# A conformer layer on one core: another order of products in the ffns' first block, and other PSUM banks for the memory values

## The chip, the cores and the metric

The kernel runs on one core of a Trainium2 chip. The metric is device time in microseconds (us); lower is better. TensorE (PE in the profile) multiplies, VectorE (DVE) and ScalarE (ACT) do elementwise work and read and write PSUM, GpSimd (POOL) makes a few powers, SyncE (SP) issues DMAs. PSUM has eight banks of 128 x 512 words; a matmul adds into one of them.

## The reference

One layer over 512 rows of 1024 columns, in float32: half a SwiGLU ffn, a mixer of three attention branches with gates, half a second ffn, a norm.

```
def swiglu(h, wg, wu, wd):
    return (jax.nn.silu(h @ wg) * (h @ wu)) @ wd

def memory_attention(q, mk, mv):
    sc = jnp.einsum('bshd,bmhd->bhsm', q, mk).astype(jnp.float32) * (d ** -0.5)
    p = jax.nn.softmax(sc, axis=-1)
    return jnp.einsum('bhsm,bmhd->bshd', p.astype(mv.dtype), mv).reshape(b, s, h * d)

x = x + 1/2 * SwiGLU(RMSNorm(x))
h = RMSNorm(x)
y = sum_i sigmoid(h W_g + b_g)_i * (o_i W_branch_i);  x = x + y W_out
x = x + 1/2 * SwiGLU(RMSNorm(x))
x = RMSNorm(x)
```

D_FF is 2816, so each ffn has 22 tiles of 128 hidden columns. Memory has 256 tokens; its keys and values are one product of the normed memory rows each, and keys and queries are normed per head.

## The kernel before

Every float32 factor is split into a high and a low half (`split`, L76 to L78: ScalarE casts, VectorE subtracts, so that "hi" is ready first and "lo" after it), and a product is three matmuls: hi by hi, lo by hi, hi by lo (`mm3`, L108 to L112).

**The ffn** (`ffn`, from L346) goes through the hidden tiles in blocks of 4, 6, 6 and 6 (`CHUNKS`). Two hidden tiles make an `Item`. Its two by two block product of gate and up weights is computed in Strassen's way, with seven products numbered 1 to 7 instead of eight. Each is 24 matmuls of 256 columns (`mm7`, L364). Their left operands are sums of parts of the normed rows (`mhi`, `mlo`), their right ones sums of weight quarters, which VectorE makes and splits (`Item.prep`, L390). Products 1, 6, 7 and 4 add one after the other to the same bank, `self.y` (tag `s`); products 5 and 3 add to `self.z` (tag `p` or `o`); product 2 has a bank of tag `g`. Between two additions to `y` the intermediate value is read out: `snap` (L415 to L418) is a ScalarE copy of the bank, after products 1, 6 and 7. The next product to the same bank waits for it. `gated` then makes silu of one part by the other, and `done` (L435) splits the result of a hidden tile into `gh` and `gl`, the operands of the down projection.

The down projection has two halves of 512 output columns (`dh`). For each, a chunk (L513 to L524) multiplies two hidden tiles: 24 matmuls of 512 columns into four banks. Chunk 0 of the first half is put ahead of the last item's products 4 and 3 (`end`).

The written order of a block is a list of jobs; `run_jobs` (L334) prepares the weights of jobs ahead of their use, as far as a ring of six weight blocks goes, and then runs the job. Each job's matmuls stand in a `tc.manual_schedule` of their own: within it TensorE's order is as written, while between jobs the framework's scheduler may put the matmuls of one job between those of another, and it does. In the first block of four tiles, with items A and B, the written order is A1 A2 B1 B2, A6 A5 A7 A4 A3, B6 B5 B7, chunk 0, B4 B3, chunk 2, then the second half's chunks. In the same block the left operands are still being made (`Operands`, rows, L201 to L250), and the memory rows are normed.

**Memory** (L618 to L651) comes between the first ffn and the mixer. `rows_product` (L584) multiplies in four chunks of weights (`mwh`, `mwl`), with accumulators for two tiles of 128 tokens. The keys' two accumulators are the two `s` banks. `norm4` (L604) takes squares (ScalarE), sums (`hss`, VectorE), a power (POOL), and scales; `heads_T` (L611) transposes the result through a `t` bank. The values' accumulators are the same two `s` banks, so their first matmul waits until the norm has read the keys. `PLAN_C0` is a list for the first step of the mixer that says in what turn projections (p), gate products (f) and the parts of memory's attention (c.qt, c.sc, ...) are issued.

Of the kernel before, what the change touches and what calls it, by code (L numbers as in the profile page):

```python
# [11 lines left out]
F32 = mybir.dt.float32  # L12
# [6 lines left out]
P = 128  # L19
# [7 lines left out]
NMT = NM // P  # L27
# [4 lines left out]

PLAN_C0 = "p2 c.qt p2 c.sc p2 f4 c.sc2 p3 f2 c.qt f2 c.pt f4 c.pv"
PLAN_C = "c.sc f1 p2 u.ot c.ot p2 u.pt c.sc2 p2 u.qt p3 c.qt f1 u.sc f1 c.pt f1 u.pv f1 c.pv"
# [13 lines left out]
def layer_kernel(ctx: ExitStack, tc: tile.TileContext, a: dict, out: bass.AP):  # L48
# [11 lines left out]
    def bank(tag):  # L60
        return pp.tile([P, 512], F32, tag=tag, name="ps_" + tag, bufs=BANKS[tag])
# [272 lines left out]
    def run_jobs(jobs, ring):  # L334

        made = alive = 0
        for n, job in enumerate(jobs):
            while made < len(jobs) and (made <= n or alive + jobs[made].blocks <= ring):
                alive += jobs[made].blocks
                jobs[made].got = jobs[made].prep() if jobs[made].prep else None  # L340
                made += 1
            with tc.manual_schedule(engines={mybir.EngineType.PE}):
                job.run(job.got)
            alive -= job.blocks

    def ffn(pre, x_sb, ops, fp, after, raws=None, before_last=None, after_half=None):  # L346
# [122 lines left out]
        ft = 0  # L469
        for n, nf in enumerate(CHUNKS):  # L470
# [4 lines left out]
            order = []  # L475
# [3 lines left out]
            else:  # L479
                order += [(items[0], 1), (items[0], 2)]  # L480
            for i, item in enumerate(items):
                order += [(item, 6), (item, 5), (item, 7)]
                if i + 1 < len(items) and not (ft == 0 and i == 0):
                    order += [(items[i + 1], 1)]
                if ft == 0 and i == 0:
                    order += [(item, 4), (item, 3)]
                elif i + 1 < len(items):
                    order += [(item, 4), (item, 3), (items[i + 1], 2)]
            jobs = [product(*o) for o in order]
# [3 lines left out]
            for dh in range(2):  # L493
# [31 lines left out]
                else:  # L525
                    run_jobs(jobs, RING)
                    jobs = []
# [83 lines left out]
    def heads_T(yn, dst, cols):  # L611

        ps = bank("t")
        for h in range(4):
            nc.tensor.transpose(ps[:, h * P:(h + 1) * P], yn[:, h * P:(h + 1) * P], ident)
        split(heads(ps, 4), dst[0][:, :, cols], dst[1][:, :, cols])
# [5 lines left out]
    mkT = [base.tile([P, 4, NM], F32R, tag="w4", name=n, bufs=2) for n in ("mkh", "mkl")]  # L622
    mk_ps = rows_product([bank("s") for _ in range(NMT)], mT, a["w_mem_kv"], 0, **mem_w)
    for t in range(NMT):
        yn = mem_pool.tile([P, 512], F32, tag="mk", name="mk", bufs=3)
        sq = mem_pool.tile([P, 512], F32, tag="mk", name="mksq", bufs=3)
        heads_T(norm4(mk_ps[t], yn, sq, gck), mkT, slice(t * P, (t + 1) * P))
    cq_ps = rows_product([bank(t) for t in ("p", "g", "g", "o")], h2, a["w_in"], 3072)
# [3 lines left out]
    for t in range(NT):  # L632
        sq = mem_pool.tile([P, 512], F32, tag="mk", name="cqsq", bufs=3)
        norm4(cq_ps[t], c_rows[:, t, :], sq, gcq)

    lam = mem_pool.tile([P, 512], F32, tag="mk", name="lam", bufs=3)
    la = lam[:, 0:256].rearrange("p (u v d) -> p u v d", u=2, v=2)
# [9 lines left out]
                            op0=ALU.add, op1=ALU.subtract)  # L647
    mv_ps = rows_product([bank("s") for _ in range(NMT)], mT, a["w_mem_kv"], 512, **mem_w)
    mv = base.tile([P, NMT, 512], F32, tag="kx", name="mv", bufs=2)
    for t in range(NMT):  # L650
        nc.scalar.copy(out=mv[:, t, :], in_=mv_ps[t])  # L651
    memp.__exit__(None, None, None)
    mix_in["mTp"].__exit__(None, None, None)
# [500 lines left out]
```

## Time and profile before

| | us |
|---|---|
| median of 3 runs | 1267.36 (1266.86 to 1268.57) |
| the profiled execution | 1268.73 |
| its span | 1266.9 |
| TensorE busy | 1228.1 (97%) |
| VectorE busy | 843.0 (67%) |
| ScalarE busy | 596.8 (47%) |

The mean granted clock of TensorE is 0.986 of full speed. The first block of the first ffn runs until 98.16 us, the memory stage from about 409 to 447 us, the first block of the second ffn from 905 to 986.5 us. Idle time in brackets at the end of a row is that of the row's engine just before the instruction, with what ended it. All times are from the span's start.

### The profile page before, as it was taken

The page shows a single profiled execution, that of the slowest core. Times are in us where ns is not written, and L with a number is a line of the kernel's source. Part 1 is how long each engine was busy: PE and PEld are TensorE (multiplying, and loading weights), DVE is VectorE, ACT ScalarE, POOL GpSimd, SP SyncE. Part 2 cuts the span into 40 slices and gives each one's busy share as a digit, 9 for nine tenths or more (in the row PEclk, how much of TensorE's full clock was granted, in tenths as well). Part 3 has the DMA queues.
Part 4 walks back from the last instruction along what each step waited for, and adds up shares of the span by engine and source line. Part 5 has one row for each costly group of instructions (what it writes and reads, how often), then busy time and mean ns, then how long its engine had stood idle before and what let it go on. Part 6 is the DMA issues. An engine that isn't in the chain of part 4 may idle for free.

```text
span 1266.9 us, 19640 instructions
## 1 busy us (share of the span) xinstructions
PE 1228.1 (97%) x7808; PEld 1119.2 (88%) x7808; DVE 843.0 (67%) x1377; ACT 596.8 (47%) x1115; POOL 106.2 (8%) x108
## 2 busy tenths in 40 slices
PE   7889999999999899999999999999989999999997
PEld 7779989989987799999999999888887998998996
DVE  7977667667664756667765664554697776766753
ACT  7534525435443455554554544442464452542543
POOL 1100000000000301111121121111000000000002
PEclk8899999999999899999999999999989999999999
DMA  6532423323333413212221321145143242332311
GB/s 222 174 103 82 135 84 107 127 79 122 102 123 117 123 39 109 88 42 84 88 88 54 93 88 38 63 146 186 34 135 115 70 134 97 101 125 76 123 44 67
DMA packets 53084, 127.57 MB, mean 101 GB/s; under 512 B 10112, under 2 KB 10624, under 8 KB 52992
## 3 DMA queue, kind: packets, MB, share of 16 engines
q1 hardware_dynamic: 52416, 125.27, 31.1%
q8 instruction: 61, 1.00, 0.3%
q10 hardware_dynamic: 576, 1.05, 0.2%
q14 instruction: 31, 0.25, 0.1%
HBM read 122.11 MB, written 4.19 MB: 100 GB/s over the span
## 4 chain that ended last, share of the span: by engine, by line
PE 91%; DVE 4%; ACT 1%; DMA 1%; POOL 1%; issue 1%; SPq 0%; POOLq 0%; DVEq 0%; ACTq 0%
PE ps_s L373 19%; PE ps_g L110 9%; PE ps_g L112 9%; PE ps_g L111 9%; PE ps_o L373 5%; PE ps_p L110 5%; PE ps_p L112 5%; PE ps_p L111 4%; PE ps_p L373 4%; PE ps_g L373 4%; PE ps_s L110 3%; PE ps_s L111 3%; PE ps_s L112 3%; PE ps_o L906 2%; PE ps_s L874 2%; PE ps_t L722 1%
## 5 line engine op out<-in xcount | busy, mean ns | idle before, releaser
L77 ACT CAST whi<-wraw 128x1024 fp32r<-128x1024 f32 (+1 forms) x120 | 119.1, 993 | 144.6 <-PE ps_s L373 74.1
L78 DVE TENSOR_TENSOR wlo<-wraw,whi 128x1024 fp32r<-128x1024 f32 (+1 forms) x120 | 137.9, 1151 | 67.8 <-ACT whi L77 65.1
L373 PE MATMUL ps_s<-mhi,whi 128*128 128x256 f32 x496 | 140.3, 283 | 8.1 <-ACT snap L417 7.9
L373 PE MATMUL ps_s<-mlo,whi 128*128 128x256 f32 x496 | 139.3, 281 | 0.0
L373 PE MATMUL ps_s<-mhi,wlo 128*128 128x256 f32 x496 | 138.3, 281 | 0.6 <-DVE wlo L78 0.6
L373 PEld LDWEIGHTS ps_s<-mhi,whi 128*128 128x128 f32 x496 | 94.6, 191 | 10.6 <-ACT snap L417 9.5
L77 ACT CAST whi<-quarter 128x1024 fp32r<-128x1024 f32 x54 | 56.8, 1052 | 96.4 <-PE ps_o L112 22.4
L373 PEld LDWEIGHTS ps_s<-mlo,whi 128*128 128x128 f32 x496 | 94.7, 191 | 0.9 <-DVE mlo L78 0.2
L373 PEld LDWEIGHTS ps_s<-mhi,wlo 128*128 128x128 f32 x496 | 94.5, 191 | 0.9 <-DVE wlo L78 0.8
L110 PE MATMUL ps_p<-whi,hh 128*128 128x384 f32 (+1 forms) x264 | 95.0, 360 | 0.0
L112 PE MATMUL ps_p<-whi,hl 128*128 128x384 f32 (+1 forms) x264 | 89.6, 340 | 0.0
L111 PE MATMUL ps_p<-wlo,hh 128*128 128x384 f32 (+1 forms) x264 | 89.0, 337 | 0.0
L78 DVE TENSOR_TENSOR wlo<-quarter,whi 128x1024 fp32r<-128x1024 f32 x54 | 66.0, 1222 | 23.9 <-ACT whi L77 23.9
L110 PE MATMUL ps_g<-hh,fh 128*128 128x512 f32 x192 | 78.1, 407 | 0.0
L112 PE MATMUL ps_g<-hh,fl 128*128 128x512 f32 x192 | 75.5, 393 | 0.1
L111 PE MATMUL ps_g<-hl,fh 128*128 128x512 f32 x192 | 74.9, 390 | 0.0
L859 DVE CAST kx<-ps_t 128x256 fp32r<-128x256 f32 x32 | 13.6, 425 | 84.6 <-PE ps_t L857 84.6
L121 POOL TENSOR_TENSOR rsh<-msh,mhalf 128x4 f32<-128x4 f32 x38 | 45.2, 1191 | 277.5 <-DVE msh L127 225.8
L78 DVE TENSOR_TENSOR fl<-wraw,fh 128x768 fp32r<-128x768 f32 x48 | 50.0, 1042 | 24.0 <-ACT fh L77 24.0
L77 ACT CAST fh<-wraw 128x768 fp32r<-128x768 f32 x48 | 39.9, 833 | 37.7 <-PE ps_g L111 22.4
L724 ACT COPY pT<-ps_t 128x512 f32<-128x512 f32 (+3 forms) x56 | 23.5, 452 | 69.3 <-PE ps_t L722 69.3
L110 PEld LDWEIGHTS ps_p<-whi,hh 128*128 128x128 f32 x264 | 50.4, 191 | 1.6
(416 smaller groups left out, 3691.7 us busy)
## 6 DMA issues: line engine op xcount, KB each, us to landing
wraw<-in_ffn_w SPq DMA_DIRECT2D x88, 512.0 KB, 3.8
wraw<-in_ffn_wd SPq DMA_DIRECT2D x44, 512.0 KB, 3.9
wraw<-in_w_u SPq DMA_DIRECT2D x32, 384.0 KB, 3.2
wraw<-in_w_gb SPq DMA_DIRECT2D x32, 384.0 KB, 3.1
wraw<-in_w_gf SPq DMA_DIRECT2D x16, 384.0 KB, 3.1
wraw<-in_w_mem_kv SPq DMA_DIRECT2D x8, 512.0 KB, 4.1
wraw<-in_w_out SPq DMA_DIRECT2D x8, 512.0 KB, 4.8
x_sb<-in_x SPq DMA_DIRECT2D x4, 512.0 KB, 7.0
```

The lines of the kernel that those rows point to most:

```text
L77: nc.scalar.copy(out=hi, in_=raw)
L78: (engine or nc.vector).tensor_tensor(out=lo, in0=raw, in1=f32(hi), op=ALU.subtract)
L110: nc.tensor.matmul(ps, lhsT=st[0], rhs=mv[0], start=first, stop=False)
L111: nc.tensor.matmul(ps, lhsT=st[0], rhs=mv[1], start=False, stop=False)
L112: return nc.tensor.matmul(ps, lhsT=st[1], rhs=mv[0], start=False, stop=last)
L121: nc.gpsimd.tensor_tensor(out=rs, in0=ms, in1=mhalf[:, :n], op=ALU.pow)
L373: nc.tensor.matmul(ps[:, c], lhsT=x, rhs=y, start=first and j + k + n == 0, stop=k == 3 and n == 2, skip_group_check=True)
L722: nc.tensor.transpose(ps[:, j * P:(j + 1) * P], pt[:, j * P:(j + 1) * P], ident)
L724: nc.scalar.copy(out=pT[:, :n * P], in_=ps[:, :n * P])
L859: nc.vector.tensor_copy(out=un.kx[:, :, qs], in_=heads(p2[:, 0:256], 2))
L874: nc.tensor.matmul(out_, lhsT=q, rhs=k, start=j == 0, stop=j == 1)
L906: nc.tensor.matmul(o[:, vs], lhsT=pT[:, j * P:(j + 1) * P], rhs=un.v[:, j, vs], start=j == 0, stop=j == i)
```

## The change

The first block's list of products is written in another order, all jobs of a list stand in one `manual_schedule`, so that TensorE follows the written order across jobs, too; the memory values accumulate in the two `t` banks, and the keys are transposed after the values' product; and the squares get buffers of their own. `PLAN_C0` is rewritten.

```diff
--- before.py
+++ after.py
@@ -30,7 +30,7 @@
 AHEAD = 600
 
 
-PLAN_C0 = "p2 c.qt p2 c.sc p2 f4 c.sc2 p3 f2 c.qt f2 c.pt f4 c.pv"
+PLAN_C0 = "p6 c.qt p3 f4 c.sc f4 c.sc2 f2 c.qt f1 c.pt f1 c.pv"
 PLAN_C = "c.sc f1 p2 u.ot c.ot p2 u.pt c.sc2 p2 u.qt p3 c.qt f1 u.sc f1 c.pt f1 u.pv f1 c.pv"
 PLAN_A = "c.sc p2 c.ot c.sc2 p3 u.pt p2 u.qt u.ot p2 c.pt f2 u.sc f1 u.pv c.pv f3"
 PLAN_B = "p5 u.pt p2 u.qt u.ot p2 f1 u.sc f1 u.pv f4"
@@ -334,14 +334,14 @@
     def run_jobs(jobs, ring):
 
         made = alive = 0
-        for n, job in enumerate(jobs):
-            while made < len(jobs) and (made <= n or alive + jobs[made].blocks <= ring):
-                alive += jobs[made].blocks
-                jobs[made].got = jobs[made].prep() if jobs[made].prep else None
-                made += 1
-            with tc.manual_schedule(engines={mybir.EngineType.PE}):
+        with tc.manual_schedule(engines={mybir.EngineType.PE}):
+            for n, job in enumerate(jobs):
+                while made < len(jobs) and (made <= n or alive + jobs[made].blocks <= ring):
+                    alive += jobs[made].blocks
+                    jobs[made].got = jobs[made].prep() if jobs[made].prep else None
+                    made += 1
                 job.run(job.got)
-            alive -= job.blocks
+                alive -= job.blocks
 
     def ffn(pre, x_sb, ops, fp, after, raws=None, before_last=None, after_half=None):
 
@@ -478,14 +478,15 @@
                 order += [(items[0], 1), (items[0], 2), (items[1], 1), (items[1], 2)]
             else:
                 order += [(items[0], 1), (items[0], 2)]
-            for i, item in enumerate(items):
-                order += [(item, 6), (item, 5), (item, 7)]
-                if i + 1 < len(items) and not (ft == 0 and i == 0):
-                    order += [(items[i + 1], 1)]
-                if ft == 0 and i == 0:
-                    order += [(item, 4), (item, 3)]
-                elif i + 1 < len(items):
-                    order += [(item, 4), (item, 3), (items[i + 1], 2)]
+            if ft == 0:
+
+                order += [(items[0], 6), (items[0], 5), (items[0], 7), (items[1], 6), (items[0], 4), (items[0], 3),
+                          (items[1], 5), (items[1], 7)]
+            else:
+                for i, item in enumerate(items):
+                    order += [(item, 6), (item, 5), (item, 7)]
+                    if i + 1 < len(items):
+                        order += [(items[i + 1], 1), (item, 4), (item, 3), (items[i + 1], 2)]
             jobs = [product(*o) for o in order]
             end = [product(items[-1], 4), product(items[-1], 3)]
 
@@ -621,19 +622,20 @@
         nc.sync.dma_start(out=g, in_=a[f"c_{n}_norm"].partition_broadcast(P))
     mkT = [base.tile([P, 4, NM], F32R, tag="w4", name=n, bufs=2) for n in ("mkh", "mkl")]
     mk_ps = rows_product([bank("s") for _ in range(NMT)], mT, a["w_mem_kv"], 0, **mem_w)
+    mk = []
     for t in range(NMT):
-        yn = mem_pool.tile([P, 512], F32, tag="mk", name="mk", bufs=3)
-        sq = mem_pool.tile([P, 512], F32, tag="mk", name="mksq", bufs=3)
-        heads_T(norm4(mk_ps[t], yn, sq, gck), mkT, slice(t * P, (t + 1) * P))
+        yn = mem_pool.tile([P, 512], F32, tag="mk", name="mk", bufs=2)
+        sq = mem_pool.tile([P, 512], F32, tag="mksq", name="mksq", bufs=2)
+        mk.append(norm4(mk_ps[t], yn, sq, gck))
     cq_ps = rows_product([bank(t) for t in ("p", "g", "g", "o")], h2, a["w_in"], 3072)
     y_sb = base.tile([P, ND, S], F32, tag="xy", name="y_sb")
 
     c_rows = y_sb[:, ND - NT:, :]
     for t in range(NT):
-        sq = mem_pool.tile([P, 512], F32, tag="mk", name="cqsq", bufs=3)
+        sq = mem_pool.tile([P, 512], F32, tag="cqsq", name="cqsq", bufs=2)
         norm4(cq_ps[t], c_rows[:, t, :], sq, gcq)
 
-    lam = mem_pool.tile([P, 512], F32, tag="mk", name="lam", bufs=3)
+    lam = mem_pool.tile([P, 512], F32, tag="cqsq", name="lam", bufs=2)
     la = lam[:, 0:256].rearrange("p (u v d) -> p u v d", u=2, v=2)
     nc.sync.dma_start(out=la, in_=a["a_lambda"].rearrange("(u v) d -> u v d", u=2).partition_broadcast(P))
     lp = heads(lam[:, 256:384], 2)
@@ -645,10 +647,12 @@
 
     nc.vector.tensor_scalar(out=nlam, in0=le[:, 1:2], scalar1=-LAMBDA_INIT, scalar2=le[:, 0:1],
                             op0=ALU.add, op1=ALU.subtract)
-    mv_ps = rows_product([bank("s") for _ in range(NMT)], mT, a["w_mem_kv"], 512, **mem_w)
+    mv_ps = rows_product([bank("t") for _ in range(NMT)], mT, a["w_mem_kv"], 512, **mem_w)
     mv = base.tile([P, NMT, 512], F32, tag="kx", name="mv", bufs=2)
     for t in range(NMT):
         nc.scalar.copy(out=mv[:, t, :], in_=mv_ps[t])
+    for t in range(NMT):
+        heads_T(mk[t], mkT, slice(t * P, (t + 1) * P))
     memp.__exit__(None, None, None)
     mix_in["mTp"].__exit__(None, None, None)
     norm_pool[0] = (base, "raw", 6)
```

With A and B the two items of the first block, the written order is now A1 A2 B1 B2, A6 A5 A7 B6 A4 A3 B5 B7, chunk 0, B4 B3, chunk 2. The order of the instructions shows three places.

TensorE at the end of the first ffn's first block, around B3's last matmuls (`ps_p`) and what follows. Before:

```order
L112 MATMUL ps_o_745<-whi_552,gl_243 128x512
L373 MATMUL ps_p_667<-mhi_64,wlo_627 128x256
L110 MATMUL ps_s_870<-ohi_695,gh_242 128x512
L111 MATMUL ps_s_870<-olo_696,gh_242 128x512
L112 MATMUL ps_s_870<-ohi_695,gl_243 128x512
L110 MATMUL ps_s_870<-ohi_695,gh_242 128x512
L111 MATMUL ps_s_870<-olo_696,gh_242 128x512
L112 MATMUL ps_s_870<-ohi_695,gl_243 128x512
L110 MATMUL ps_p_871<-ohi_695,gh_242 128x512
L111 MATMUL ps_p_871<-olo_696,gh_242 128x512
```

And after the change:

```order
L373 MATMUL ps_p_637<-mhi_64,wlo_597 128x256
L373 MATMUL ps_p_637<-mhi_64,whi_596 128x256
L373 MATMUL ps_p_637<-mlo_65,whi_596 128x256
L373 MATMUL ps_p_637<-mhi_64,wlo_597 128x256
L110 MATMUL ps_g_706<-fhi_633,gh_242 128x512
L111 MATMUL ps_g_706<-flo_634,gh_242 128x512
L112 MATMUL ps_g_706<-fhi_633,gl_243 128x512
L110 MATMUL ps_g_706<-fhi_633,gh_242 128x512
```

`ohi` is chunk 0 of the second half of columns, `fhi` is chunk 2 of the first half. Before, chunk 0 of the second half stood between B3 and chunk 2; now chunk 2 follows B3 directly.

VectorE in the same block, up to the low half of B6's weights (before it is flo_443, after the change wlo_363; `quarter` holds sums of weights, `xn` is the norm of memory rows). Before:

```order
L78 TENSOR_TENSOR mlo_65<-gl_126,mhi_64 128x1024
L141 SCALAR_TENSOR_TENSOR xn_3927<-mt_3917,rs_3925,gain_3888 128x512 x2
L78 TENSOR_TENSOR wlo_321<-quarter_318,whi_320 128x1024
L78 TENSOR_TENSOR wlo_361<-wraw_268,whi_360 128x1024
L399 TENSOR_TENSOR quarter_434<-wraw_436,wraw_438 128x1024
L78 TENSOR_TENSOR wlo_397<-quarter_282,whi_396 128x1024
L400 TENSOR_TENSOR quarter_435<-quarter_434,wraw_252 128x1024
L409 TENSOR_TENSOR quarter_509<-wraw_252,wraw_436 128x1024
L78 TENSOR_TENSOR olo_476<-quarter_434,ohi_475 128x1024
L422 TENSOR_TENSOR cc_543<-ps_o_483,snap_541 128x512
L405 TENSOR_TENSOR quarter_479<-wraw_258,quarter_435 128x1024
L78 TENSOR_TENSOR flo_443<-quarter_435,fhi_442 128x1024
```

And after the change:

```order
L409 TENSOR_TENSOR quarter_317<-wraw_74,wraw_268 128x1024
L433 TENSOR_TENSOR pr_426<-sg_427,cc_424 128x256
L78 TENSOR_TENSOR mlo_65<-gl_126,mhi_64 128x1024
L156 TENSOR_SCALAR ms_3647<-ss_3643 128x1
L78 TENSOR_TENSOR wlo_320<-quarter_317,whi_319 128x1024
L141 SCALAR_TENSOR_TENSOR xn_3651<-mt_3641,rs_3649,gain_3612 128x512 x2
L399 TENSOR_TENSOR quarter_354<-wraw_356,wraw_358 128x1024
L400 TENSOR_TENSOR quarter_355<-quarter_354,wraw_254 128x1024
L409 TENSOR_TENSOR quarter_493<-wraw_254,wraw_356 128x1024
L78 TENSOR_TENSOR olo_463<-quarter_354,ohi_462 128x1024
L405 TENSOR_TENSOR quarter_466<-wraw_260,quarter_355 128x1024
L78 TENSOR_TENSOR wlo_363<-quarter_355,whi_362 128x1024
```

Before, the low halves of A4's and A3's weights (wlo_361 and wlo_397) stood ahead of B6's; now B6's comes ahead of theirs, since B6 stands ahead of A4 and A3 on TensorE.

VectorE in the memory stage, around the low half of the keys (`mkl`), the low half of the first queries (`cql`) and the scaling of `ga`, a gain that is loaded by a DMA. Before:

```order
L640 TENSOR_TENSOR lam_4422<-lam_4422 128x128
L78 TENSOR_TENSOR mkl_4146<-ps_t_4250,mkh_4145 128x4x128
L127 TENSOR_SCALAR msh_4416<-hss_4414 128x4
L602 TENSOR_TENSOR y_sb_4381<-ps_g_4259,rsh_4408 128x512
L642 TENSOR_REDUCE mhalf_87<-lam_4422 128x2
L608 TENSOR_TENSOR y_sb_4381<-y_sb_4381,gcq_4142 128x512
L602 TENSOR_TENSOR y_sb_4381<-ps_o_4260,rsh_4418 128x512
L646 TENSOR_SCALAR mhalf_87<-mhalf_87 128x1
L608 TENSOR_TENSOR y_sb_4381<-y_sb_4381,gcq_4142 128x512
L78 TENSOR_TENSOR cql_4579<-ps_t_4580,cqh_4578 128x512
L673 TENSOR_SCALAR gsub_4514<-gsub_4514 128x128
L679 TENSOR_SCALAR ga_4518<-ga_4518 128x64
```

And after the change:

```order
L603 TENSOR_TENSOR y_sb_4094<-ps_o_3973,rsh_4131 128x512
L609 TENSOR_TENSOR y_sb_4094<-y_sb_4094,gcq_3869 128x512
L648 TENSOR_SCALAR mhalf_87<-mhalf_87 128x1
L609 TENSOR_TENSOR y_sb_4094<-y_sb_4094,gcq_3869 128x512
L677 TENSOR_SCALAR gsub_4241<-gsub_4241 128x128
L78 TENSOR_TENSOR fl_4356<-wraw_4353,fh_4355 128x768
L683 TENSOR_SCALAR ga_4245<-ga_4245 128x64
L78 TENSOR_TENSOR fl_4394<-wraw_4391,fh_4393 128x768
L78 TENSOR_TENSOR mkl_3873<-ps_t_4218,mkh_3872 128x4x128
L683 TENSOR_SCALAR gb_4244<-gb_4244 128x64
L78 TENSOR_TENSOR mkl_3873<-ps_t_4225,mkh_3872 128x4x128
L78 TENSOR_TENSOR cql_4318<-ps_t_4319,cqh_4317 128x512
```

Before, both halves of mkl stood ahead of gsub and ga (the first of the two is nine rows above the piece shown); now both stand behind ga, and behind two splits of gate weights (`fl`).

## Rows read from the trace of the kernel before

**Rows 1.** The page's first part: busy time, share of the span, instructions.

```profile
PE 1228.1 (97%) x7808; PEld 1119.2 (88%) x7808; DVE 843.0 (67%) x1377; ACT 596.8 (47%) x1115; POOL 106.2 (8%) x108
```

**Rows 2.** The table of TensorE's waits: total us, times, longest.

```profile
PE ps_s L373 <- ACT snap L417: 7.9, 8, 1.5
PE ps_s L110 <- DVE mk L602: 5.8, 1, 5.8
...
PE ps_o L373 <- DVE mlo L78: 3.5, 2, 3.2
```

**Rows 3.** Windows of both ffns' first blocks; the head row names the columns.

```profile
core 0: us, PE busy (x) PEld busy (x) DVE busy (x) ACT busy (x) POOL busy (x), PEclk, DMA share, GB/s
30.00:40.00 10.00, 5.67 (x27) 4.60 (x26) 9.56 (x12) 5.40 (x9) 4.86 (x1) 0.70 0.35 106
60.00:70.00 10.00, 6.99 (x59) 6.59 (x58) 9.22 (x13) 5.75 (x9) 0.00 (x0) 1.00 0.64 209
80.20:98.16 17.96, 17.31 (x76) 13.61 (x75) 13.51 (x17) 4.20 (x5) 0.00 (x0) 1.00 0.09 30
925.00:935.00 10.00, 6.83 (x35) 6.63 (x35) 10.00 (x12) 6.95 (x9) 0.00 (x0) 0.66 0.28 96
```

**Rows 4.** Timeline of TensorE, first ffn: start, us, instruction, idle before and its end.

```profile
38.12 0.58 PE L373 MATMUL ps_o<-mlo,whi 128*128 128x256 f32 x1 [0.36 <-DVE mlo L78]
...
45.92 0.39 PE L373 MATMUL ps_s<-mhi,whi 128*128 128x256 f32 x1 [0.92 <-ACT snap L417]
...
52.11 0.38 PE L373 MATMUL ps_s<-mhi,whi 128*128 128x256 f32 x1 [0.44 <-ACT snap L417]
...
64.71 0.39 PE L373 MATMUL ps_s<-mhi,whi 128*128 128x256 f32 x1 [1.51 <-ACT snap L417]
...
69.23 0.39 PE L373 MATMUL ps_s<-mhi,whi 128*128 128x256 f32 x1 [1.51 <-ACT snap L417]
```

**Rows 5.** Timeline of VectorE, same block.

```profile
34.91 1.42 DVE L141 SCALAR_TENSOR_TENSOR xn<-mt,rs,gain 128x512 f32<-128x512 f32 x2 [0.44 <-POOL rs L121]
...
39.45 0.69 DVE L78 TENSOR_TENSOR mlo<-quarter,mhi 128x512 fp32r<-128x512 f32 x1
...
45.77 1.22 DVE L78 TENSOR_TENSOR wlo<-quarter,whi 128x1024 fp32r<-128x1024 f32 x1
46.91 1.22 DVE L78 TENSOR_TENSOR wlo<-wraw,whi 128x1024 fp32r<-128x1024 f32 x1
```

**Rows 6.** Timelines around the end of that block's last product.

```profile
80.17 0.28 PE L373 MATMUL ps_p<-mhi,wlo 128*128 128x256 f32 x1
80.28 0.39 PE L110 MATMUL ps_s<-ohi,gh 128*128 128x512 f32 x1
...
84.14 0.50 PE L110 MATMUL ps_g<-fhi,gh 128*128 128x512 f32 x1 [0.46 <-ACT gh L77]
...
83.47 0.62 ACT L77 CAST gh<-pr 128x512 fp32r<-128x512 f32 x1 [0.99 <-DVE pr L433]
```

**Rows 7.** Timeline of TensorE, second ffn's first block.

```profile
928.85 0.58 PE L373 MATMUL ps_o<-mlo,whi 128*128 128x256 f32 x1 [3.17 <-DVE mlo L78]
...
969.54 0.39 PE L112 MATMUL ps_o<-whi,gl 128*128 128x512 f32 x1
```

**Rows 8.** Memory: windows, VectorE and ScalarE instructions, the DMA (KB, us to landing).

```profile
408.90:447.40 38.50, 31.42 (x147) 25.42 (x146) 28.17 (x57) 19.11 (x38) 11.83 (x13) 0.91 0.48 126
415.00:420.00 5.00, 5.00 (x13) 3.93 (x14) 3.84 (x9) 1.20 (x2) 1.80 (x2) 0.54 0.21 72
...
410.42 0.68 DVE L600 TENSOR_REDUCE hss<-mksq 128x4 f32<-128x512 f32 x1
411.02 1.22 DVE L78 TENSOR_TENSOR mwl<-wraw,mwh 128x1024 fp32r<-128x1024 f32 x1
...
424.91 1.28 ACT L643 ACT_TABLE_LOAD   x1
...
ga<-in_a_q_norm SPq DMA_DIRECT2D x1, 32.0 KB, 6.3
```

## The prediction, made before the result was known

> **What bounds the kernel now.** I read the page's busy times first, then the table of waits, then windows of the three places that the diff touches, and last single instructions there. TensorE is busy for 97% of the span [rows 1]. So the time is TensorE's work, plus its idle time, plus what half clock costs. The table of waits says what idle time there is to win [rows 2]: 7.9 us before products that add to a bank whose copy ("snap") isn't taken yet, eight times; 5.8 us at once before memory's values, whose first product needs a bank that VectorE's norm of the keys still reads; and 3.5 us on a split that VectorE hadn't made.
>
> The windows tell which of these waits is really the one that ends last [rows 3]. In the first ffn TensorE is busy for 5.67 of 10 us in 30:40, where VectorE is busy for 9.56. In 60:70 it is busy for 6.99, with VectorE at 9.22. In the second ffn's 925:935 VectorE has no free time at all and the clock is 0.66. So through most of the first block VectorE sets the pace: it makes the low halves and the sums of the weights. A wait on a bank that goes away there is in part only a wait on VectorE a little later. From 80.20 to 98.16, the down projections, TensorE idles for 0.65 us in 17.96 [rows 3].
>
> **The first block of the first ffn.** Its jobs now run on TensorE strictly as written. Gone are its four snap waits, 0.92, 0.44, 1.51 and 1.51 [rows 4], 4.4 us of the 7.9 [rows 2]. New are three waits on VectorE's list.
>
> First, product 6 stands where 5 stood. It needs the second half of its left operand. In the old list that half's split ended at 39.45 + 0.69 = 40.1 [rows 5], after one 1.14 us sum; in the new one a weight split stands ahead too, so about 41.2, where product 5 had gone on at 38.12 [rows 4].
>
> Second, product 6 of the second item stands straight behind 7. It needs wlo_363, which the second excerpt in the section on the change shows at the end of twelve rows. With one split ahead of them they take, by starts in the trace, ten times 1.14 us (45.77 to 46.91 [rows 5]), a pair of norm halves at 1.33 us (listed 1.42 [rows 5]), and some 0.5 us of small ones: 13.2 us, with a wait for a POOL power as before (0.44 [rows 5]) some 13.6, so 41.2 + 13.6 = 54.8. TensorE has by then done 6, 5 and 7, each 24 matmuls of 256 columns at 0.113 us (80.17 to 80.28 [rows 6]), 2.72 us, with about 1.5 us at half clock: 41.2 + 8.2 + 1.5 = 50.9. It idles for 3.9 us. Behind that wait follow 4, 3, 5, 7 (10.9 us), the chunk of the down projection (24 at 17.31 / 76 = 0.227 us [rows 3], 5.45 us) and 4 and 3 (5.45 us): with 1 to 1.5 us of half clock the last product ends at 54.8 + 2.7 + 21.8 + 1.3 = 80.6 to 80.9, where it ended at 80.17 + 0.28 [rows 6]. So the snap waits' gain is spent on VectorE: +0.4 us.
>
> The third place is dearer. Chunk 2 of the down projection multiplies what product 3 of the second item gates. Before, the scheduler had put half a chunk of the other 512 columns in between (first excerpt); it covered the way from the last product at 80.45 through sum and gate to the cast at 83.47 and a first matmul at 84.14, a wait of 0.46 us [rows 6], of 0.65 us idle in the whole stretch [rows 3]. In the new order chunk 2 stands straight behind product 3. The same path is 84.14 - 80.28 = 3.9 us (counted from where the next instruction followed the last product), all of it idle. That is 3.9 - 0.65 = +3.2 us; the chunk that covered it now comes later, at its full price.
>
> After an idle time of such a length the clock may fall. Bounds from rows: nothing, since the 1.51 us waits at 64.71 and 69.23 lie in a window with clock 1.00 [rows 3, 4]; and 2.0 us, since in 415:420, behind the 5.78 us wait, 13 products were started at clock 0.54 where 22 fit at 0.227 [rows 8]. I take 1.5, nearer to the second, as 3.9 us of idle time lies between 1.5 and 5.8. The Trainium skill, "TensorE: Matmul & The Clock Gate" (section "Why this matters for your kernels"), warns of idle gaps above some 3 us between bursts of matmuls; by it each of the new long waits costs a slow stretch, and the sum would be by 0.5 us higher for each of the two waits before a chunk 2, and by up to 2 us for each of the others; 928.85, with 3.17 us ahead of it and 0.66 in its window, agrees [rows 3, 7].
>
> First ffn: 0.4 + 3.2 + 1.5 = **+5.1 us**.
>
> **The first block of the second ffn.** The same order and the same lists. The other four of the eight snap waits, 7.9 - 4.4 = 3.5 us [rows 2, 4], go. Product 6 starts half a microsecond after where product 5 did (928.85, a wait that stays [rows 7]); 6 behind 7 finds its split some 3 us late by the same list. The last product and the chunk behind it would end at about 969.2; before, the scheduler's order had both done at 969.54 + 0.23 = 969.8 [rows 7], so -0.6. Then the wait before chunk 2, which wasn't there before: +3.9 (VectorE's list holds a 1.14 us split in between, as in the first ffn), and +1.5 of clock. Together **+4.8 us**. In the other three blocks of each ffn the written order leaves two products or a whole chunk between a result and its use, 5 us and more: nothing.
>
> **Memory.** The values get banks of their own, so the 5.78 us go, and the 2.0 us at half clock behind it; the stretch 408.90:447.40 has 7.08 us idle in all [rows 8]. In its place:
> - four reductions of 0.68 us (0.60 from start to start) now stand ahead of the second low half of the values' weights, where one stood; it ended at 411.02 + 1.22 = 412.24 and ends now at 414.05, and TensorE, which started the values at about 409.5, wants it one chunk of 2.7 us later, at 412.2 [rows 8]: 1.85 us;
> - the projection that the order puts into the last chunk waits for the norm that frees its bank: about 1.0;
> - the transposes of the second keys' tile need a bank that the second copy of the values frees, and a table load of 1.28 us stands ahead of that copy [rows 8]: 1.0;
> - the transposes of the first queries need a bank that the low half of the keys frees, and in VectorE's new list (third excerpt) this stands behind the scaling of ga, a DMA. SP issues that DMA behind a load whose slot the last low half frees, at about 422.2, so at 423.0; it landed 6.3 us after its issue [rows 8]: 429.3, then a scaling of 0.2, a split of 0.95 and the half itself: 430.9. TensorE is there at about 427.5: 3.4 us;
> - the second scores wait some 0.85.
>
> That is 8.1 us of idle time for 7.1, and +1.0 of clock for -2.0: **0 us**. Bounds: -7.8, if nothing takes the place of the wait, and +3, if the clock falls twice.
>
> **Sum.** 5.1 + 4.8 + 0 = +9.9 us. The profiled execution took 1268.73 (span 1266.9), so 1278.6 on it; the median lies 1.4 lower, at 1267.36, which gives **1277**.
>
> **Rivals.**
> 1. Faster: memory's whole wait goes (-7.8), and the snap waits are real gains, as VectorE makes up its lag; the two waits before chunk 2 stay. -7.8 - 7.9 + 3.2 + 3.9 = -8.6 without a fall of the clock, so 1258.8. For it: VectorE isn't full in the chunks (13.51 of 17.96 [rows 3]). Against it: 9.22 to 10.00 of 10 busy before that [rows 3]. It decides if product 6 of the second item starts without a wait.
> 2. No change: memory gains its 7.8, the ffns lose as forecast: -7.8 + 9.9 = +2.1, 1269.5. For it: 5.78 is the longest single wait, and ga's DMA may land sooner in a quieter queue. It decides if the first queries' transposes don't wait.
> 3. Slower still: every new wait of 3 us or more is followed by 2.0 us of lost clock, as behind the 5.78 us [rows 8]: 0.5 more for each chunk 2, 1.0 more in memory, 0.7 and 2.0 more behind product 6 of the second items, 4.7 in all: 1282. The Trainium skill's rule on gaps, in the section named above, would make this the time. Against it: part of the first block ran at half clock before, too (0.70 in 30:40 [rows 3]), and that part may go.
>
> **How the numbers follow.** Forecast 0.51, rival 1 0.17, rival 2 0.13, rival 3 0.19; the forecast has the most because the place of chunk 2 is certain from the order, and rival 1 the least of the two large ones because VectorE is full where it needs room. A measurement of this kernel tells 0.2%, 2.5 us, from no change. Faster has rival 1: 0.17. Same has rival 2 where it comes out under 1269.9, and a little of the forecast's lower side: 0.11. The rest is slower: 0.72. Alone, the forecast reaches from 1272 to 1281. The range takes in rival 2, most of rival 3 and the edge of 1: 1261 to 1283.
>
> **What would show it.** In the new profile: no waits on "snap" in either first block; a wait of about 4 us on a weight's low half before product 6 of the second item; one of 3 to 5 us on the gated result ("gh" or "gl") where chunk 2 starts, in both ffns; a wait of 2 us and more on "mkl" before the transposes of the first queries. If chunk 2 doesn't wait, the forecast is wrong; if product 6 doesn't, its half for the snaps is.

## The result, and the profile after

The changed kernel takes 1282.57 us (median of 4 runs, 1282.04 to 1282.76), the kernel before 1267.11 us in the same comparison: a ratio of 1.0122, with an interval of 1.0110 to 1.0134, or 15.5 us more. The forecast was 1277, 9.9 us more, with a range to 1283. The direction was right, the sum was two thirds of what came, and the time lies just inside the range.

The table of TensorE's waits (total us, times, longest), of the changed kernel:

```profile
PE ps_g L110 <- ACT gh L77: 7.7, 2, 3.9
PE ps_s L373 <- DVE mlo L78: 6.7, 4, 3.6
PE ps_t L201 <- DVE xn L141: 5.9, 3, 3.3
PE ps_s L373 <- DVE wlo L78: 5.8, 2, 3.0
PE ps_s L373 <- ACT mhi L77: 4.8, 1, 4.8
PE ps_t L616 <- DVE mkl L78: 2.6, 1, 2.6
PE ps_t L111 <- DVE mwl L78: 1.8, 1, 1.8
```

It answers to [rows 2]. The 7.9 us on "snap" and the 5.8 us on "mk" are gone. In their place stand 7.7 us before chunk 2 of the two first blocks (gh), 5.8 us before product 6 of the second item (wlo), and more waits for the left operands (mlo, mhi). Memory's one wait became three, 2.6, 1.8 and 1.1 us; the ffns' eight snap waits became longer ones of other names.

The timeline of TensorE in the first ffn (start, us, instruction; in brackets idle time before it and what ended it):

```profile
35.13 0.58 PE L373 MATMUL ps_s<-mhi,ohi 128*128 128x256 f32 x1 [4.80 <-ACT mhi L77]
...
41.23 0.58 PE L373 MATMUL ps_s<-mlo,ohi 128*128 128x256 f32 x1 [2.44 <-DVE mlo L78]
...
55.02 0.39 PE L373 MATMUL ps_s<-mhi,wlo 128*128 128x256 f32 x1 [2.85 <-DVE wlo L78]
...
85.59 0.80 PE L110 MATMUL ps_g<-fhi,gh 128*128 128x512 f32 x1 [3.86 <-ACT gh L77]
```

and in the second:

```profile
949.67 0.38 PE L373 MATMUL ps_s<-mhi,wlo 128*128 128x256 f32 x1 [2.95 <-DVE wlo L78]
...
980.15 0.50 PE L110 MATMUL ps_g<-fhi,gh 128*128 128x512 f32 x1 [3.86 <-ACT gh L77]
```

Product 6 goes on at 41.23, where 5 went on at 38.12 [rows 4]. Product 6 of the second item waits until 55.02 for the last row of the second excerpt. Chunk 2 waits 3.86 us behind the last product, in both ffns. Before, other matmuls stood there: in the first ffn half of the other columns' chunk 0 [rows 6], in the second nearly the whole of chunk 0 [rows 7] and then such a half.

Windows of the changed kernel (columns as in [rows 3]):

```profile
30.00:40.00 10.00, 2.85 (x12) 1.99 (x11) 9.56 (x12) 6.94 (x10) 5.92 (x1) 0.63 0.32 102
40.00:50.00 10.00, 8.77 (x56) 8.78 (x57) 9.53 (x12) 4.30 (x8) 1.39 (x1) 0.68 0.40 143
50.00:60.00 10.00, 7.15 (x49) 6.96 (x48) 9.55 (x11) 6.36 (x9) 0.00 (x0) 0.83 0.69 229
80.00:92.00 12.00, 8.14 (x33) 6.59 (x32) 6.39 (x9) 2.65 (x5) 0.00 (x0) 0.72 0.28 87
```

In 30:40 TensorE is busy for 2.85 us where it was for 5.67 [rows 3], and VectorE's 9.56 us are the same to the digit: VectorE sets the pace there. Behind the wait for chunk 2 the clock is low: 0.72 in 80:92, where 80.20:98.16 had 1.00 before [rows 3].

Windows from the first ffn's first product to the start of the last matmul of the block's products, of the kernel before and then of the changed one:

```profile
16.35:80.17 63.82, 54.50 (x382) 51.23 (x380) 57.77 (x69) 37.23 (x58) 7.79 (x3) 0.89 0.47 153
16.25:81.44 65.19, 53.81 (x381) 51.32 (x380) 58.54 (x68) 36.82 (x57) 8.93 (x3) 0.85 0.46 148
```

TensorE idled for 9.3 us in it before and for 11.4 us after, without one wait on snap: what the new order took away came back under other names, and more.

Memory, changed kernel:

```profile
422.47 0.50 PE L111 MATMUL ps_t<-mwl,mh 128*128 128x512 f32 x1 [1.77 <-DVE mwl L78]
...
435.17 0.66 PE L616 MATMUL ps_t<-ident,mk 128*128 128x128 f32 x4 [1.07 <-ACT mv L653]
...
438.46 0.80 PE L616 MATMUL ps_t<-ident,y_sb 128*128 128x128 f32 x4 [2.64 <-DVE mkl L78]
```

To see where the time lies I cut every profiled execution at the same places: a stage runs from its first product to the first of the next (memory: from the first matmul with mwh, the keys' product included, to the first product of probabilities and values). The mixer behind memory takes 465.4 to 465.5 us in all five profiles of this table and is left out. The first kernel was profiled three times and the changed one twice, since single profiles of one kernel differ. In us:

| | ffn 1, first block | ffn 1, later blocks | memory | ffn 2, first block | ffn 2, later blocks |
|---|---|---|---|---|---|
| before | 81.6, 81.7, 80.9 | 296.5, 296.5, 296.4 | 52.9, 52.3, 53.2 | 73.5, 72.1, 72.4 | 273.4 (all) |
| after | 88.4, 87.3 | 298.1, 297.9 | 51.0, 50.8 | 79.5, 79.4 | 275.1, 274.8 |
| difference of the means | +6.4 | +1.5 | -1.9 | +6.8 | +1.5 |

The differences add to 14.3; the rest of the 15.5 is within the spread of single profiles (spans of before 1264.9 to 1266.9, of after 1279.2 and 1280.9).

### The profile page after: what moved, and what is told of

Same layout as the page of the kernel before. It is cut to its first block, busy times and chain, and to the rows that moved or that the text cites. A ratio compares the mean times of both kernels' runs of the same rounds, so it can differ in the third digit from the quotient of the medians.

```text
span 1280.9 us, 19652 instructions
## 1 busy us (share of the span) xinstructions
PE 1233.1 (96%) x7808; PEld 1121.9 (88%) x7808; DVE 846.6 (66%) x1377; ACT 599.1 (47%) x1115; POOL 108.5 (8%) x108
## 4 chain that ended last, share of the span: by engine, by line
PE 87%; DVE 7%; DMA 2%; ACT 2%; issue 1%; POOL 1%; SPq 0%; POOLq 0%; DVEq 0%; ACTq 0%
PE ps_s L373 17%; PE ps_g L110 9%; PE ps_g L112 9%; PE ps_g L111 9%; PE ps_o L373 5%; PE ps_p L110 5%; PE ps_p L112 5%; PE ps_p L111 4%; PE ps_p L373 4%; PE ps_g L373 4%; PE ps_s L110 2%; PE ps_s L112 2%; PE ps_s L111 2%; PE ps_o L910 2%; PE ps_s L878 2%
## 5 line engine op out<-in xcount | busy, mean ns | idle before, releaser
L373 PE MATMUL ps_s<-mhi,wlo 128*128 128x256 f32 x512 | 144.6, 282 | 5.8 <-DVE wlo L78 5.8
L373 PE MATMUL ps_s<-mlo,whi 128*128 128x256 f32 x512 | 144.5, 282 | 0.6 <-DVE mlo L78 0.6
L373 PE MATMUL ps_s<-mhi,whi 128*128 128x256 f32 x512 | 144.6, 282 | 0.3 <-ACT whi L77 0.3
L373 PEld LDWEIGHTS ps_s<-mhi,wlo 128*128 128x128 f32 x512 | 98.3, 192 | 6.2 <-DVE wlo L78 6.2
L373 PEld LDWEIGHTS ps_s<-mhi,whi 128*128 128x128 f32 x512 | 98.6, 193 | 1.1 <-ACT whi L77 0.5
L373 PEld LDWEIGHTS ps_s<-mlo,whi 128*128 128x128 f32 x512 | 97.8, 191 | 1.7 <-DVE mlo L78 1.2
L121 POOL TENSOR_TENSOR rs<-ms,mhalf 128x1 f32<-128x1 f32 x18 | 17.2, 955 | 420.4 <-DVE ms L156 357.2
```

The source lines that it names most:

```text
L121: nc.gpsimd.tensor_tensor(out=rs, in0=ms, in1=mhalf[:, :n], op=ALU.pow)
L373: nc.tensor.matmul(ps[:, c], lhsT=x, rhs=y, start=first and j + k + n == 0, stop=k == 3 and n == 2, skip_group_check=True)
```

## The experiments

All are compared with the kernel before on the same chip; "over" is the median's difference from its median there (1266.31 in the first four, 1266.68 in the next four).

| kernel | median us | ratio, interval | over, us |
|---|---|---|---|
| e1_memory | 1268.05 | 1.0016 (1.0007 to 1.0025) | +1.7 |
| e2_list | 1269.91 | 1.0026 (1.0016 to 1.0037) | +3.6 |
| e3_schedule | 1287.45 | 1.0166 (1.0151 to 1.0181) | +21.1 |
| e5_end_first | 1276.11 | 1.0075 (1.0063 to 1.0088) | +9.8 |
| e6_order | 1278.79 | 1.0098 (1.0085 to 1.0111) | +12.1 |
| e7_fill | 1279.22 | 1.0102 (1.0087 to 1.0116) | +12.5 |
| e8_first_only | 1276.81 | 1.0083 (1.0071 to 1.0095) | +10.1 |
| e9_five_first | 1270.26 | 1.0032 (1.0019 to 1.0044) | +3.6 |

and their stages, one profile each:

| | ffn 1, first | ffn 1, later | memory | ffn 2, first | ffn 2, later |
|---|---|---|---|---|---|
| e1_memory | 80.5 | 296.5 | 51.8 | 75.1 | 273.4 |
| e2_list | 82.5 | 296.4 | 52.1 | 75.9 | 273.4 |
| e3_schedule | 91.1 | 298.1 | 51.9 | 82.2 | 275.0 |
| e5_end_first | 85.6 | 298.4 | 51.0 | 76.6 | 275.0 |
| e6_order | 87.3 | 298.2 | 51.7 | 76.7 | 275.3 |
| e7_fill | 85.8 | 298.4 | 52.8 | 77.8 | 275.4 |
| e8_first_only | 86.1 | 296.5 | 52.2 | 79.5 | 273.4 |
| e9_five_first | 82.4 | 296.5 | 52.8 | 75.1 | 273.4 |

Memory's -1.9 us in the table above is the difference of five profiles only. All six profiles with the old memory part lie between 51.9 and 53.2 us (mean 52.5), all seven with the new one between 50.8 and 52.8 (mean 51.6), which makes the gain 0.9.

### One part alone: memory, the list, the schedule

**e1_memory** keeps the ffn of before and takes the memory part and PLAN_C0 of the changed kernel:

```diff
-    mv_ps = rows_product([bank("s") for _ in range(NMT)], mT, a["w_mem_kv"], 512, **mem_w)
+    mv_ps = rows_product([bank("t") for _ in range(NMT)], mT, a["w_mem_kv"], 512, **mem_w)
...
+    for t in range(NMT):
+        heads_T(mk[t], mkT, slice(t * P, (t + 1) * P))
```

> Only the memory part and PLAN_C0, the ffn as before. Theory A (what the two traces say: the memory stage took 1.9 us less, everything else is the ffns' loss): 1265.2 us against 1267.1, with waits of about 1.8 us on mwl, 1.1 on the copy of the values and 2.6 on mkl in place of 5.8 on mk. Rival B (the forecast's sum: new waits take the whole gain): 1267.1. Rival C (the gain is lost again behind the stage or the stage meets other DMA traffic when it comes 8 us earlier): 1268 or more.

Measured: 1.7 us over. Rows of its waits:

```profile
PE ps_t L615 <- DVE mkl L78: 2.6, 1, 2.6
...
PE ps_t L111 <- DVE mwl L78: 1.7, 1, 1.7
...
PE ps_t L615 <- ACT mv L652: 1.1, 1, 1.1
```

The three waits are the expected ones, and the memory stage is shorter by some 0.9 us against the mean of before. Yet the kernel isn't faster. The second ffn's first block, whose code it doesn't touch, takes 75.1 us where before took 72.1 to 73.5: the order of VectorE's instructions in that block differs, and TensorE has all of chunk 0 ahead of the last product there, where before had two of its matmuls. I take it that the scheduler places a whole program and the edit upstream shifts what it thinks is ready. So theory A holds for the stage and fails for the total; C was right about the total, for another reason than the one it gave. With one profile this cause is likely, not shown. The banks and PLAN_C0 changed together here, and no run separates them.

**e2_list** has the new list, and a schedule for each job as before (the edit is the second half of the diff's ffn part):

> Only the new list of products, every job in a schedule of its own as before; the scheduler puts half of the other columns' chunk 0 ahead of chunk 2 again. Theory A (one schedule over the whole list is what costs, since it keeps that filler out): 1266 to 1269 us, no wait over 1 us before chunk 2. Rival B (the new list costs, by product 6 of the second item that waits on VectorE and the half clock behind it): 1271 to 1274, with that wait of about 3 us there.

Measured: 3.6 us over, 1269.91. Rows of its waits:

```profile
PE ps_s L373 <- ACT snap L417: 5.0, 4, 1.5
...
PE ps_s L373 <- DVE wlo L78: 2.2, 1, 2.2
...
PE ps_g L110 <- ACT gh L77: 0.9, 2, 0.5
```

Chunk 2 hardly waits (0.9 us in both ffns), as theory A has it; snap waits of 5.0 us stay, since the scheduler moves the products of different jobs again. Of B's wait for product 6 of the second item, 2.2 us came, in the first ffn alone. The total lies a little over A's figures and under B's: the list alone costs a little.

**e3_schedule** has the old list in one schedule:

```diff
+        with tc.manual_schedule(engines={mybir.EngineType.PE}):
+            for n, job in enumerate(jobs):
...
                 job.run(job.got)
```

> Only the one schedule over each list, with the old list of products. Theory A: the wait of 3.9 us before chunk 2 and 1.5 to 2.0 us of half clock in both ffns (+10.5 in all, less the 0.65 that before had) and 3.3 us in the blocks of six tiles: 1279 to 1282 us. Rival B (the new list costs): 1267 to 1272 us.

Measured: 21.1 us over, more than the changed kernel itself. Timeline of TensorE in its first ffn:

```profile
68.04 0.50 PE L110 MATMUL ps_g<-whi,gh 128*128 128x512 f32 x1 [2.02 <-ACT gh L77]
...
71.21 0.79 PE L112 MATMUL ps_g<-whi,gl 128*128 128x512 f32 x1 [2.44 <-DVE gl L78]
...
88.44 0.80 PE L110 MATMUL ps_g<-fhi,gh 128*128 128x512 f32 x1 [3.86 <-ACT gh L77]
```

The wait of 3.86 us before chunk 2 is there with the old list, so it is the one schedule's. I had not expected that chunk 0 waits as well, 2.0 and 2.4 us: under the strict order nothing fills in for it either. Theory A is right about the cause and too low in the price; B is out. The changed kernel, at 15.5, is 5.6 us better, but it differs from this one by the memory part as well as by the list. By stages, its first blocks are shorter by 3.3 and 2.8 us (means of 87.8 and 79.4 against 91.1 and 82.2) and its memory by 1.0; this profile is the longest of four runs. So most of the 5.6 us is the new list's, but only in a kernel that is already locked to its written order.

### Chunk 2 and its clock

**e5_end_first**: the changed kernel with the second item's products 4 and 3 ahead of chunk 0 in the first block.

```diff
+                    if dh == 0 and ft == 0:
+                        jobs += end
                     for k in range(0, nf, 2):
...
-                        if dh == 0 and k == 0:
+                        if dh == 0 and k == 0 and ft > 0:
                             jobs += end
```

> The changed kernel, but in the first block products 4 and 3 of the second item stand ahead of chunk 0, which then covers the way to chunk 2. Theory A: the waits of 3.86 us before chunk 2 and the half clock behind them go (4.0 + 2.0 and 4.0 + 1.5, 11.5 us), and product 4 behind 7 waits for its snap (1.5 us, twice): 1282.6 - 11.5 + 3.0 = 1274 us. Rival B (chunk 0 waits instead, or the clock falls anyway): 1279 or more.

Measured: 9.8 us over, 5.7 less than the changed kernel (by ratios, 1.0075 against 1.0122). The wait before chunk 2 is gone, and in the first ffn the clock is 1.00 from 70 to 102 us. Two rows of its waits say what came:

```profile
PE ps_s L373 <- ACT snap L417: 3.0, 2, 1.5
...
PE ps_p L373 <- DVE cc L422: 1.8, 2, 1.0
```

The snap waits of product 4 behind 7 are back, 3.0 us as expected, and product 3 waits 1.8 us for a bank that VectorE's sum frees. 11.5 - 3.0 - 1.8 leaves 6.7 us; 5.7 came. So the chunk's wait and the clock behind it together cost about what theory A said, within some 1 us. Which of the two costs what, this run doesn't tell; the next one does.

**e7_fill** puts 32 needless matmuls into that gap:

```diff
+        def fill():
+            ps = bank("t")
+            for k in range(32):
+                nc.tensor.matmul(ps[:, :HS], lhsT=identr, rhs=M[1][0][:, k % 4, :], start=k == 0, stop=k == 31)
...
                         if dh == 0 and k == 0:
                             jobs += end
+                            if ft == 0:
+                                jobs.append(Job(None, lambda blk: fill(), 0))
```

> The changed kernel with 32 needless matmuls of 256 columns (3.6 us at full clock, into a free bank, their result is never read) between product 3 of the second item and chunk 2, in both ffns. They stand where TensorE idles for 3.86 us. Theory A (the idle time lets the clock fall, which cost 2.0 and 1.5 us in the chunk behind it): the clock stays at 1.00 there and 3 to 3.5 us come back: 1279 us. Rival B (the clock falls for another reason, or those slow matmuls are slow by waits): no change, 1282.6, or longer by what the fill overlaps.

Measured: 1279.22 (four runs, 1277.59 to 1281.45), 12.5 us over against 15.5. The intervals of the two ratios overlap a little, so the totals alone don't settle it; the trace does. Windows around the gap (columns as in [rows 3]), of the changed kernel and then of the one with the fill:

```profile
82.00:84.00 2.00, 0.00 (x0) 0.00 (x0) 1.73 (x3) 1.53 (x3) 0.00 (x0) 0.96 0.78 231
84.00:86.00 2.00, 0.41 (x1) 0.41 (x2) 1.32 (x3) 0.62 (x1) 0.00 (x0) 0.50 0.09 35
86.00:88.00 2.00, 2.00 (x6) 1.48 (x6) 0.26 (x1) 0.00 (x0) 0.00 (x0) 0.50 0.00 0
```

```profile
82.00:84.00 2.00, 2.00 (x19) 2.00 (x18) 1.99 (x3) 0.81 (x2) 0.00 (x0) 1.00 0.74 238
84.00:86.00 2.00, 2.00 (x18) 1.95 (x17) 0.86 (x2) 0.86 (x2) 0.00 (x0) 1.00 0.03 12
86.00:88.00 2.00, 2.00 (x10) 1.61 (x9) 0.81 (x2) 1.10 (x4) 0.51 (x1) 1.00 0.04 8
```

With nothing in the gap the clock is at its lower level of 1.2 GHz (0.50) when chunk 2 starts: 6 matmuls in 2 us. With the fill it stays at 1.00, and 10 matmuls go through in a stretch of equal length. In the second ffn the clock is 0.50 in 982:984 without the fill and 1.00 throughout 977:987 with it. From chunk 2's first matmul to the next block's first product, 72 matmuls in every case, the changed kernel takes 19.0 and 18.3 us in the first ffn (two profiles) and 18.5 twice in the second; with the fill it takes 16.7 and 16.9, which is 2.0 and 1.6 us less than the means. Theory A is shown: the half clock behind the idle time is a price of its own, of about that size. One more thing moved: eight transposes of memory rows (0.8 us), at 36.85 us in the changed kernel, stand behind the fill and ahead of chunk 2 here; they lie outside that measure. The memory stage of this profile is 1.9 us longer than the changed kernel's; its granted clock is 0.94 there (400.5:453.3) against 0.97 (402.7:453.7), which is some 1.6 us of it, as an estimate from the two shares.

### The later blocks

**e8_first_only**: one schedule for the first block's list only.

```diff
-            run_jobs(jobs, RING)
+            run_jobs(jobs, RING, ft == 0)
```

(with `whole` as a third argument, that chooses between one schedule and one for each job.)

> The changed kernel, but only the first block's list stands in one schedule; in the blocks of six tiles every job has its own, as before. Theory A (the strict order costs 3.3 us in the six later blocks, where chunk 4 stands too close behind the last product, and the scheduler used to put the other columns' chunk 0 ahead): 1279.3 us. Rival B (those 3.3 us are the trace's or come from another place): 1282.6.

Measured: 1276.81, 10.1 us over. The later blocks are back at 296.5 and 273.4 us, as in every kernel that leaves them to the scheduler, and the five kernels that lock them, the changed one among them, have 297.9 to 298.4 and 274.8 to 275.4. So the lock costs 2.9 to 3.9 us there, and theory A is right about the blocks and about the size. A window over block 2 of the first ffn shows TensorE without a gap:

```profile
98.00:189.00 91.00, 91.00 (x650) 85.16 (x649) 62.47 (x73) 38.85 (x54) 0.00 (x0) 1.00 0.32 105
```

In the changed kernel the same block has short waits where chunk 4 starts. The starts of TensorE's rows there are 0.33 to 0.39 us apart where 0.23 is usual:

```profile
174.09 0.40 PE L112 MATMUL ps_p<-ohi,gl 128*128 128x512 f32 x1
174.45 0.50 PE L110 MATMUL ps_g<-whi,gh 128*128 128x512 f32 x1
174.79 0.40 PE L111 MATMUL ps_g<-wlo,gh 128*128 128x512 f32 x1
175.18 0.50 PE L112 MATMUL ps_g<-whi,gl 128*128 128x512 f32 x1
175.52 0.40 PE L110 MATMUL ps_g<-whi,gh 128*128 128x512 f32 x1
```

Chunk 4 is the one with whi and gh. The last matmul of the product that it needs, and the cast of its operand's high half:

```profile
168.60 0.28 PE L373 MATMUL ps_o<-mhi,flo 128*128 128x256 f32 x1
...
173.78 0.62 ACT L77 CAST gh<-pr 128x512 fp32r<-128x512 f32 x1 [1.59 <-DVE pr L433]
```

The cast ends at 174.40, 5.7 us after the product (168.72, where the next matmul followed it), and the other columns' chunk between the two, 24 matmuls, is over by then: here the chunk doesn't cover the way. That is 0.5 us of the 0.9 that this block lost. The rest is spread over its 504 matmuls of 256 columns, which start 0.9 ns further apart; no run shows why. The total fell by more than the later blocks give (5.4 us by the medians), and under both theories' figures. The profile of this run, the longest of five, is 3.4 us shorter than the mean of the changed kernel's two: 3.1 in the later blocks, 1.7 in the first ffn's first block, whose list and lock are the same, and memory 1.3 longer. The other 2 us no profile shows.

### Other orders

**e6_order**: as e5_end_first, with product 3 of the first item between 7 and 4 of the second, so that no two products in a row share a bank:

```diff
-                order += [(items[0], 6), (items[0], 5), (items[0], 7), (items[1], 6), (items[0], 4), (items[0], 3),
-                          (items[1], 5), (items[1], 7)]
+                order += [(items[0], 6), (items[0], 5), (items[0], 7), (items[1], 6), (items[0], 4), (items[1], 5),
+                          (items[1], 7), (items[0], 3)]
```

> The changed kernel with another list in the first block: product 3 of the first item stands between 7 and 4 of the second, and 4 and 3 of the second item stand ahead of chunk 0, so that no two products in a row share a bank and chunk 2 has its cover. Theory A (bank waits are real time when nothing else is late): the 3.0 us of snap waits of the kernel with 4 and 3 ahead (9.8 us over the kernel before) go: 1273 us against 1266.3 of that comparison. Rival B (VectorE sets the pace of the block, a bank wait that goes away becomes a wait on a low half): 1275 to 1277.

Measured: 12.1 us over, 1278.79, worse than with the two snap waits and than either theory's figure. Rows of its waits:

```profile
PE ps_g L110 <- ACT gh L77: 6.3, 4, 3.0
...
PE ps_g L112 <- DVE gl L78: 3.7, 2, 2.1
```

No bank wait is left, and 10 us of waits for gated results have come: product 3 now stands too close ahead of chunk 0, two products later, 5.4 us, while VectorE has a queue (9.77 of 10 us busy in 70:80, where these waits lie in the first ffn). Rival B was right that the wait only changes its name, though what is late is the result and not a weight's half.

**e9_five_first**: memory as before, the lock in the first block only, product 5 first and 4 and 3 of the second item ahead of chunk 0.

The main line of the edit (the preparation of weights also makes the sums for 5 ahead of those for 6, and the schedule is that of e8_first_only):

```diff
+                order += [(x, 5), (x, 6), (x, 7), (y, 5), (x, 4), (y, 6), (x, 3), (y, 7)]
```

> A candidate: memory as before, one schedule in the first block only, with the list 1 2 of both, 5 6 7 of the first item, 5 of the second, 4, 6 of the second, 3, 7 4 3 of the second, chunk 0, chunk 2. Product 5 comes first since its operands are complete sooner than those of 6. Theory A (VectorE sets the pace of the first block, and the place of 6 and of the second item's first products decides how well TensorE is covered): the loss of each first block is 0 to 1.5 us, 1266 to 1269 against 1266.3. Rival B (any strict order in the first block loses, since the scheduler's interleaving of products is what hides VectorE): 1271 or more.

Measured: 1270.26, 3.6 us over. It is the best of the locked kernels, between the two theories: its first blocks cost 1.0 and 2.4 us over the mean of before (82.4 and 75.1 us). A written order can come near the scheduler's; none that I tried beats it. No kernel here is faster than the one before.

### The same kernels once more

p1_before_again and p3_before_third are the kernel before, p2_after_again the changed kernel, without an edit, each for one profile.

> The kernel before, profiled once more. The two profiles so far differ by 14.0 us of span, the medians by 15.5 and more. If the profile of before fell on one of its longer runs, this one is 1 to 2.5 us shorter (span 1264.5 to 1266), and the stage that is shorter tells where runs of one kernel differ; if not, span 1266.9 and all stages equal within 0.2 us.

> The changed kernel, profiled once more. If the first block of an ffn has no fixed time from run to run, its stage differs by 1 us or more from the 88.35 and 79.45 us of the first profile; if it has, all stages agree within 0.2 us and the span is 1280.9.

> The kernel before, a third profile, for the spread of each stage: the same two expectations as for the second profile of it.

Measured: spans of 1264.9, 1279.2 and 1265.4 us. The first profile of before was one of its longer runs, and so was that of the changed kernel. The first table above has the stages: the later blocks repeat to 0.3 us, the first blocks and memory don't. Of the changed kernel's first blocks, that of the first ffn differs by 1.1 us between its two profiles, that of the second by 0.1.

## Why the prediction was right, and where its sizes were off

- **The wait before chunk 2** was forecast from the order alone at 3.9 us. It measured 3.86 in both ffns. This step carried the forecast, and e3_schedule and e5_end_first show that its cause is the strict order.
- **The clock behind it**: 1.5 us forecast for each, about 2.0 and 1.6 by e7_fill. The row it was taken from, the half clock behind memory's 5.78 us, was a fair measure.
- **The first blocks up to the last product** were forecast at +0.4 and -0.6 and came out at about +1.4 and +0.8 against the means of before. In the first ffn VectorE's list was read rightly: product 6 came at 41.23 (41.2 forecast) and the second item's at 55.02 (54.8). Its wait was 2.85, not 3.9, since the three products ahead of it lay longer at half clock: 0.68 in 40:50, where before had the row below. The last product's last matmul began at 81.44, not 80.3 to 80.6. What was mis-sized is the clock behind 55.02 (0.83 in 50:60) and, in the second ffn, the base: the profile of before that I worked from had 73.5 us there, the two others 72.1 and 72.4, so the gain of -0.6 was reckoned against a long run. In all the first blocks cost 13.2 us by the means, 9.9 forecast.

```profile
40.00:50.00 10.00, 8.46 (x57) 8.05 (x57) 9.56 (x12) 6.29 (x10) 1.39 (x1) 0.84 0.52 173
```

- **The later blocks** were the step that failed: "5 us and more: nothing". They cost 3.0 us by the means (2.9 to 3.9 in the kernels that lock them), and e8_first_only, which doesn't, shows that it is the lock. A distance of 5.45 us isn't enough where the path from product to chunk takes 5.7 us with VectorE's queue, as at chunk 4; I had taken the 3.9 us of one place for all. That accounts for a part only; the cause of the rest stays open.
- **Memory** was forecast at 0 and came out 1.9 us shorter in the changed kernel (0.9 over all profiles). Of the five waits on the list four were there: 1.77 (1.85 forecast), 1.07 (1.0), 2.64 (3.4), and 0.3 for the scores (0.85); the projection's 1.0 didn't come. By the stages this gain hides a part of what the later blocks cost, and that is luck: 1282.57 is 0.4 us short of the range's upper end.
- **The rivals**: 1 and 2 asked that a wait be absent which was there (product 6, the first queries). Rival 3's 1282 is nearest to the median, in part only by its reason: the clock behind chunk 2 gave 0.6 us more than forecast (1.0 by the rival), memory nothing more (1.0), the first blocks up to the last product 2.4 more (2.7 behind product 6), some of it the base and not the clock; and the later blocks' 3.0 us were not in it.
- The rule that the Trainium skill ("TensorE: Matmul & The Clock Gate", section "Why this matters for your kernels") gives on idle gaps agrees with this trace: the gaps of 3.86 us were followed by a clock of 0.50. A fall followed shorter waits as well: behind those of 1.07 and 2.64 us in memory, 440:445 has 0.77.

## What to carry to other kernels

A wait on a bank that stands beside another engine at 95% may not be time to be won: here 7.9 us of such waits were taken away and came back under that engine's name. Before a scheduler's freedom is replaced by a written order, look for what the scheduler had put between a result and its use, since that filler is what the lock takes out; test the lock with the old order by itself (here +21.1 us) before judging the new order. When two profiles are compared by stages, take each kernel's profile two or three times first.

## What I had not expected of the hardware

First blocks of one and the same kernel can differ by 1 us and more between runs, and the clock goes with it: in the second ffn's 930:940 the three profiles of before have 0.75, 0.94 and 0.85, and the block takes 73.5, 72.1 and 72.4 us. The later blocks of before agree to 0.05 us. A row of the first profile of before, then two of the second:

```profile
930.00:940.00 10.00, 9.68 (x63) 9.47 (x62) 10.00 (x12) 4.79 (x6) 0.00 (x0) 0.75 0.50 159
...
920.00:930.00 10.00, 6.87 (x53) 6.66 (x53) 9.92 (x11) 8.11 (x11) 0.00 (x0) 0.89 0.16 52
930.00:940.00 10.00, 9.24 (x72) 8.83 (x72) 9.71 (x11) 5.94 (x8) 0.00 (x0) 0.94 0.44 159
```

72 matmuls were started in 930:940 there; in the first profile, at 0.75, 63. The wait ahead of that stretch, for product 5's left operand, is alike: 3.17, 3.13 and 3.15 us. So a like idle time is followed by half clock for a shorter or a longer time.
